# A hybrid decoder block in fp32 on one core: start, eviction, query pass, compressed values, gate terms and residual loads rearranged

## The chip, the core and the metric

The kernel runs on one core of a Trainium2 chip. The metric is the device time of one launch in microseconds (us), the median of several runs. The engines are PE (matrix products), DVE (VectorE), ACT (ScalarE), POOL (GpSimd) and SP (SyncE, which here issues most DMA transfers). PEld is PE's loading of stationary operands, which overlaps its products.

## What is computed

One layer, for a sequence of 1024 rows of 1024 values in fp32:

```python
h = rms_norm(x, norm_mix)
q, kv, g_attn, u_pool, g_merge = split(h @ w_in)   # 512, 768, 24, 512, 2048 columns
a = nsa_attention(q, kv, g_attn, ...) @ w_branch_attn
b = pool_mixer(u_pool, pool_w, pool_scale) @ w_branch_pool
ga, gb = split(sigmoid(g_merge))                    # 1024 each
x = x + (ga * a + gb * b) @ w_out
h = rms_norm(x, norm_mlp)
out = x + square(relu(h @ w_ff1)) @ w_ff2
```

The attention has 8 heads of 64 in 2 key groups and three branches, each with a softmax: over 63 compressed blocks of keys and values, over selected blocks, and over a window of 512 positions; the sum is weighted by gates per head. (With 16 of 16 blocks selected, the selected branch covers all earlier positions.) Queries and keys are rotated (rope).

## The kernel before

Every fp32 operand is split into a high part and a low part (`hi`, and `lo` = operand - `hi`, both float32r), and a product is the sum of three: hi by hi, hi by lo, lo by hi (`mm3`, L74 to L79; which line is which depends on the operand that stays). A tile has 128 partitions; `NT` = `NK` = 8 tiles of tokens and of channels. Weights stream through `load` (L164): a raw tile of 128x512 (256 KB; a ring of `RAWS` = 4), its high part on ACT, its low part on DVE or POOL (rings of `HILO` = 3). The order of instructions on each engine comes from a scheduler that works on the program order.

The stages, by the times of the trace: the first projection (0 to 52, L233 to L254) multiplies the normalised input by 512 key and value columns, eight PSUM banks `acc`, one for each token tile. At its end the banks are evicted (L265 to L271): ACT writes 384 columns to `kvA`, DVE reads the other 128 twice to write the high and low part of the values `vst[0]`. Block 2 (280 more columns) and `compress` follow (to 104); block 2's PSUM tiles take the banks of `acc`, so its first product needs banks that are read out. Then the queries (104 to 158): `qblock(0)` and `qblock(1)`, 256 columns each; each tile is evicted by ACT, rotated by POOL (five operations), and stored to DRAM (`qd`). The rotated keys of a tile are transposed by PE in between. From 158 to 339 come the pooling mixer and the gate products `gb` (to DRAM, `gbd`).

The attention (339 to 706, L512 to L742) runs over 32 pairs of (query tile i, head pair hp). For each, `units_a` makes scores and softmax, `units_b` transposes the probabilities (L652), splits them (ACT L655, DVE L656) and multiplies by values into `oacc` (L663); the last block of each unit is that of the compressed values, `vch`, which has 64 partitions. A pair's `units_b` runs one pair behind. Between these steps stand terms of another product: `ga_terms`, 128 terms of three products each (`psG`), whose sixteen results `z` go to DRAM (`tad`); `advance` gives them out in proportion to the work done. Query tiles come back from `qd` through `load_q` and are transposed and split (`split_q`, L549).

The attention-branch projection (706 to 745 for the first half of the sequence) multiplies `oT` by `w_branch_attn`, reads `tad` and `gbd` back and merges. Then `w_out` (first half 745 to 789, second half to 870): for each of 8 output tiles m two weight tiles, 24 products, and the residual sum on DVE (L820) with `x`, which was loaded straight into `acc[:, m, sl]` (named `accx` in the profile, L817). From 870 on the MLP runs. Besides, POOL's DMA queue makes sums of MLP weights in DRAM during the attention (`wsw_ff`, 1 MB each).

## Time and profile before

| | us |
|---|---|
| median of 3 runs | 1493.94 (1491.46 to 1497.39) |
| the profiled execution | 1493.06 |
| its span | 1491.3 |
| PE busy | 1443.1 (97%) |
| DVE busy | 1006.1 (67%) |
| ACT busy | 759.2 (51%) |
| POOL busy | 154.1 (10%) |

The span runs from the first to the last instruction of the profiled execution; 1.8 us of its time lie outside. Busy PE time contains the tails of products, which overlap the next one, so the distance from one product's start to the next, the pitch, tells more than its duration. A row of the timeline gives start, duration, engine, line, operation, output and inputs, and in brackets the idle time before it and what ended it.

### The profile page before, as it was taken

To read this page: it belongs to the slowest core of one execution; us is meant where nothing else is said; L and a number is where in the kernel's file an instruction comes from. 1 tells how busy PE (TensorE), PEld (TensorE's weight loads), DVE (VectorE), ACT (ScalarE), POOL (GpSimd) and SP (SyncE) were. 2 spreads that over 40 slices of the span, in tenths; PEclk is the share of its full clock that TensorE was granted. 3 is DMA by queue.
4 is the path that set the end of the run, shared out by engine and by line. 5 is a ranking of instruction groups with operands and counts; after the bars stand their busy time and mean duration, and the time that the engine had idled before them with its cause. 6 is when DMAs were issued, how large, how long until landed. Compare 5 with 4: busy or idle time off the path is not lost.

```text
span 1491.3 us, 20797 instructions
## 1 busy us (share of the span) xinstructions
PE 1443.1 (97%) x7385; PEld 1193.7 (80%) x7385; DVE 1006.1 (67%) x1950; ACT 759.2 (51%) x1559; POOL 154.1 (10%) x214
## 2 busy tenths in 40 slices
PE   8899999998999999999899999999999999999996
PEld 6788888886778887787688888888888888888885
DVE  5793461115888888787657658667897376669995
ACT  4454231124778877776334454575344454764451
POOL 2006423331111111111000000000000000000000
PEclk9999999999999999999999999999999999999998
DMA  8234217875768678766955332333233233333323
GB/s 309 69 100 149 71 43 189 215 202 132 201 156 212 153 187 196 171 169 150 327 174 162 108 97 91 100 100 99 85 106 97 94 99 93 99 94 97 98 80 113
DMA packets 130233, 204.67 MB, mean 137 GB/s; under 512 B 9936, under 2 KB 62928, under 8 KB 129616
## 3 DMA queue, kind: packets, MB, share of 16 engines
q1 hardware_dynamic: 112064, 136.22, 29.7%
q0 software_dynamic: 17920, 67.11, 19.9%
q8 instruction: 58, 0.95, 0.2%
q14 instruction: 47, 0.39, 0.1%
q10 hardware_dynamic: 144, 0.00, 0.0%
HBM read 186.52 MB, written 83.89 MB: 181 GB/s over the span
## 4 chain that ended last, share of the span: by engine, by line
PE 87%; DVE 5%; DMA 3%; ACT 2%; issue 1%; POOL 0%; SPq 0%; DVEq 0%; ACTq 0%; POOLq 0%
PE psm L79 16%; PE psm L77 16%; PE psm L78 16%; PE oacc L663 6%; PE psF L78 5%; PE psF L79 5%; PE psF L77 5%; PE psT L652 4%; PE psS L557 3%; PE psS L558 2%; PE psG L77 2%; PE psG L78 2%; PE psG L79 2%; DMA gb<-gbd 1%; PE psS L560 1%
## 5 line engine op out<-in xcount | busy, mean ns | idle before, releaser
L77 PE MATMUL psm<-mv,whi 128*128 128x512 f32 x896 | 350.6, 391 | 0.0
L78 PE MATMUL psm<-mv,whi 128*128 128x512 f32 x896 | 350.6, 391 | 0.0
L79 PE MATMUL psm<-mv,wlo 128*128 128x512 f32 x896 | 350.5, 391 | 0.0
L866 ACT CAST whi<-wraw 128x512 fp32r<-128x512 f32 x224 | 138.9, 621 | 257.6 <-PE psm L78 193.0
L82 DVE TENSOR_TENSOR wlo<-wraw,whi 128x512 fp32r<-128x512 f32 x288 | 196.7, 686 | 90.7 <-ACT whi L866 70.0
L78 PEld LDWEIGHTS psm<-mv,whi 128*128 128x128 f32 x896 | 168.3, 188 | 36.8
L77 PEld LDWEIGHTS psm<-mv,whi 128*128 128x128 f32 x896 | 168.3, 188 | 36.7
L79 PEld LDWEIGHTS psm<-mv,wlo 128*128 128x128 f32 x896 | 168.3, 188 | 36.7
L179 ACT CAST whi<-wraw 128x512 fp32r<-128x512 f32 x112 | 69.7, 622 | 122.2 <-PE psF L78 57.9
L656 DVE TENSOR_TENSOR pl<-psT,ph 128x512 fp32r<-128x512 f32 (+1 forms) x160 | 101.9, 646 | 30.3 <-ACT ph L655 29.0
L655 ACT CAST ph<-psT 128x512 fp32r<-128x512 f32 (+1 forms) x160 | 87.7, 556 | 49.4 <-PE psT L652 47.6
L567 DVE TENSOR_REDUCE nm<-psS 128x1 f32<-128x64 f32 (+8 forms) x192 | 99.8, 539 | 17.4 <-PE psS L560 10.2
L82 POOL TENSOR_TENSOR wlo<-wraw,whi 128x512 fp32r<-128x512 f32 x48 | 65.5, 1367 | 120.3 <-ACT whi L179 100.0
L77 PE MATMUL psF<-xh,whi 128*128 128x512 f32 x192 | 74.7, 389 | 0.0
L78 PE MATMUL psF<-xl,whi 128*128 128x512 f32 x192 | 74.7, 389 | 0.0
L79 PE MATMUL psF<-xh,wlo 128*128 128x512 f32 x192 | 74.7, 389 | 0.0
L568 ACT ACTIVATE pS<-psS,nm 128x64 f32<-128x64 f32 (+8 forms) x128 | 67.9, 532 | 8.8 <-DVE nm L567 8.3
L846 ACT CAST mv<-mt 128x512 fp32r<-128x512 f32 x96 | 59.1, 617 | 15.9 <-DVE mt L844 11.4
L82 DVE TENSOR_TENSOR mv<-mt,mv 128x512 fp32r<-128x512 f32 x96 | 65.0, 684 | 1.1 <-ACT mv L846 0.6
L663 PE MATMUL oacc<-ph,vst 128*128 128x256 f32 x264 | 64.0, 317 | 1.2 <-ACT ph L655 0.9
L652 PE MATMUL psT<-cf,pS 128*128 128x128 f32 x352 | 60.5, 276 | 2.7 <-DVE pS L624 2.6
L77 PE MATMUL psF<-bhi,xh 128*128 128x256 f32 (+1 forms) x192 | 55.6, 293 | 5.7 <-DVE vst L270 4.4
(248 smaller groups left out, 2970.0 us busy)
## 6 DMA issues: line engine op xcount, KB each, us to landing
wraw<-wsw_ff SPq DMA_DIRECT2D x128, 256.0 KB
wraw<-in_w_ff SPq DMA_DIRECT2D x96, 256.0 KB
wsw_ff<-in_w_ff POOLq DMA_DIRECT2D x16, 1024.0 KB, 9.1
wsw_ff<-wsw_ff POOLq DMA_DIRECT2D x16, 1024.0 KB, 9.5
wraw<-in_w_in SPq DMA_DIRECT2D x40, 256.0 KB
wraw<-in_w_out SPq DMA_DIRECT2D x32, 256.0 KB
xt<-in_x SPq DMA_DIRECT2D x8, 512.0 KB
qd<-q SPq DMA_DIRECT2D x16, 256.0 KB
```

Of the source, the lines that this page charges most:

```text
L77: nc.tensor.matmul(ps, lhsT=sh, rhs=mh, start=first and i == 0, stop=False, skip_group_check=more)
L78: nc.tensor.matmul(ps, lhsT=sh, rhs=ml, start=False, stop=False, skip_group_check=more)
L79: nc.tensor.matmul(ps, lhsT=sl, rhs=mh, start=False, stop=last and i == n - 1, skip_group_check=more)
L82: eng.tensor_tensor(lo, src, f(hi), op=SUB)
L179: nc.scalar.copy(h, v)
L567: nc.vector.tensor_reduce(nm, v, axis=AX.X if flat else AX.XY, op=MAX, negate=True)
L568: nc.scalar.activation(p if flat else p.rearrange("p (a n) -> p a n", a=2), v, AF.Exp, bias=nm, accum_out=sm)
L652: nc.tensor.transpose(ps[:, j, e], src[e][:, c0:c0 + P], ident)
L655: nc.scalar.copy(ph[:, :n], ps[:, :n])
L656: nc.vector.tensor_tensor(pl[:, :n], ps[:, :n], f(ph[:, :n]), op=SUB)
L663: nc.tensor.matmul(o, lhsT=v, rhs=part[:rows, j], start=gi == 0 and j == 0 and part is ph, stop=2 * gi + j == nb - 1 and part is pl)
L866: nc.scalar.copy(hi, raw)
```

## The change

- **Start.** Nine products of a constant tile with itself are put at PE's head (L235, into the last bank, which is overwritten later). The weight load of the first channel tile goes out on ACT's DMA queue, so that SP's begins with the input. The low part `wl` is subtracted by DVE, not by POOL.
- **Eviction.** ACT evicts all 512 columns of a bank to `kvA`; DVE makes the values' two parts from `kvA`.
- **Queries.** One `qblock` of 512 columns; seven of its weight tiles in a pool of their own (`qb`), one in the stream's ring. The space is that of `compress`'s tiles, now in a pool `xp` that is closed before. The keys of tile t are rotated and transposed after query tile t. POOL's ropes get buffers of their own.
- **Compressed values.** `vch` has 128 partitions, the upper half zero, so all value products read 128 rows.
- **Attention's start and end.** The first two query tiles are loaded during the pooling stage, into a pool outside (`qp`). `advance` gives 20 terms ahead at once (`FIRST`) and holds 16 back (`LAST`), of which 0.4 x 16 fall to each of the last two pairs.
- **Residual.** `x` is loaded to a tile of the ring `wraw`, which the residual sum reads.

```diff
...
 
-    def rope(eng, v, nh, cos, sin, wk):
+    def rope(eng, v, nh, cos, sin, wk, tag=""):
         cb = cos[:, None, None, :].to_broadcast([P, nh, 2, 8])
         sb = sin[:, None, :].to_broadcast([P, nh, 8])
-        A = wk.tile([P, 8, 2, 8], F32, name="ropeA", bufs=2)[:, :nh]
-        B = wk.tile([P, 8, 2, 8], F32, name="ropeB", bufs=2)[:, :nh]
+        A = wk.tile([P, 8, 2, 8], F32, name="ropeA" + tag, bufs=2)[:, :nh]
+        B = wk.tile([P, 8, 2, 8], F32, name="ropeB" + tag, bufs=2)[:, :nh]
         x = v[:, :, 0:16].rearrange("p h (b e) -> p h b e", b=2)
...
             else:
-                hi = blk.tile([P, 280], F32R, tag="bhi", name="bhi", bufs=10)
-                lo = blk.tile([P, 280], F32R, tag="blo", name="blo", bufs=10)
+                hi = blk.tile([P, n], F32R, tag="bhi", name="bhi", bufs=8 if n < HALF else 7)
+                lo = blk.tile([P, n], F32R, tag="blo", name="blo", bufs=8 if n < HALF else 7)
             v, h, l = raw[:, :w], hi[:, :w], lo[:, :w]
...
     vst = [vk.tile([P, NT, NG, P], F32R, name=f"vst{b}") for b in range(2)]
-    vch = vk.tile([DH, NG, P], F32R, name="vch")
+    vch = vk.tile([P, NG, P], F32R, name="vch")
+    nc.gpsimd.memset(f(vch[DH:P]), 0.0)
     kds = vk.tile([P, NG, NCB + S], F32R, name="kds")
...
         acc = [ps0.tile([P, HALF], F32, name="acc0") for _ in range(NT)]
+        for _ in range(9):
+            nc.tensor.matmul(acc[NT - 1][:, 0:P], lhsT=ones, rhs=ones, start=True, stop=True)
         for k in range(NK):
...
             wl = pa.tile([P, HALF], F32R, name="wl", bufs=3)
-            nc.sync.dma_start(wr, a["w_in"][k * P:(k + 1) * P, C_KC:C_KC + HALF])
+            (nc.scalar if k == 0 else nc.sync).dma_start(wr, a["w_in"][k * P:(k + 1) * P, C_KC:C_KC + HALF])
             if k == 0:
...
             nc.scalar.copy(wh, wr)
-            sub(nc.gpsimd, wl, wr, wh)
             for h in range(2):
...
                                                op0=MUL, op1=SUB)
+                if h == 0:
+                    sub(nc.vector, wl, wr, wh)
             for t in range(NT):
...
             rc = rcol[:, t:t + 1]
-            nc.scalar.activation(kvA[:, t, 0:384], acc[t][:, 0:384], AF.Copy, scale=rc)
-            vv = acc[t][:, 384:512].rearrange("p (g d) -> p g d", g=NG)
-            nc.vector.tensor_scalar(vst[0][:, t, :, 0:DH], vv, rc, None, op0=MUL)
-            nc.vector.scalar_tensor_tensor(vst[0][:, t, :, DH:P], vv, rc, f(vst[0][:, t, :, 0:DH]),
-                                           op0=MUL, op1=SUB)
+            nc.scalar.activation(kvA[:, t], acc[t], AF.Copy, scale=rc)
+            vv = kvA[:, t, 384:512].rearrange("p (g d) -> p g d", g=NG)
+            nc.vector.tensor_copy(vst[0][:, t, :, 0:DH], vv)
+            sub(nc.vector, vst[0][:, t, :, DH:P], vv, vst[0][:, t, :, 0:DH])
 
...
         wkA = pool(st, "wkA", side="right")
+        xctx = ExitStack()
+        xp = pool(xctx, "xp", side="right")
 
         def compress(kv):
-            X = wkA.tile([P, 16, NG, NCB], F32, name="X")
-            Xh = wkA.tile([P, 16, NG, NCB], F32R, name="Xh")
-            Xl = wkA.tile([P, 16, NG, NCB], F32R, name="Xl")
+            X = xp.tile([P, 16, NG, NCB], F32, name="X")
+            Xh = xp.tile([P, 16, NG, NCB], F32R, name="Xh")
+            Xl = xp.tile([P, 16, NG, NCB], F32R, name="Xl")
             nc.gpsimd.memset(X[DH:P, :, :, NCB - 1:NCB], 0.0)
...
                 for g in range(NG):
-                    nc.vector.tensor_copy(vch[:, g], f(vh[g * DH:(g + 1) * DH]))
+                    nc.vector.tensor_copy(vch[0:DH, g], f(vh[g * DH:(g + 1) * DH]))
 
...
 
-        def qblock(b):
-            w = block_w(b * 256, 256)
+        def qblock():
+            w7 = load(cols(a["w_in"], C_Q, HALF, 0, 7), nc.vector, qb)
+            w1 = load(cols(a["w_in"], C_Q, HALF, 7, 1), nc.vector)
+            w = [Parts(w7[e].tiles + w1[e].tiles) for e in range(2)]
             for t in range(NT):
...
                 ps = psF.tile([P, HALF], F32, name="psF")
-                mm3(ps[:, :256], [(XH[k][:, sl], XL[k][:, sl], w[0][:, k], w[1][:, k])
-                                  for k in range(NK)])
-                q = wkA.tile([P, 4, 2, DH], F32, name="q", bufs=2)
-                nc.scalar.activation(q, dup(ps[:, :256].rearrange("p (h d) -> p h d", d=DH)), AF.Copy,
-                                     scale=req[:, t:t + 1])
-                rope(nc.gpsimd, q.rearrange("p h e d -> p (h e) d"), 8, cosT[:, t], sinT[:, t], wkA)
-                nc.sync.dma_start(qd[t][:, b * 512:(b + 1) * 512], q.rearrange("p h e d -> p (h e d)"))
-                if b == 0:
-                    keys(t, 0, kds[:, :, NCB + t * P:NCB + (t + 1) * P])
-                elif t in (2, 5):
+                mm3(ps, [(XH[k][:, sl], XL[k][:, sl], w[0][:, k], w[1][:, k]) for k in range(NK)])
+                for b in range(2):
+                    q = wkA.tile([P, 4, 2, DH], F32, name="q", bufs=2)
+                    nc.scalar.activation(q, dup(ps[:, b * 256:(b + 1) * 256].rearrange("p (h d) -> p h d", d=DH)),
+                                         AF.Copy, scale=req[:, t:t + 1])
+                    rope(nc.gpsimd, q.rearrange("p h e d -> p (h e) d"), 8, cosT[:, t], sinT[:, t], wkA, "q")
+                    nc.sync.dma_start(qd[t][:, b * 512:(b + 1) * 512], q.rearrange("p h e d -> p (h e d)"))
+                keys(t, 0, kds[:, :, NCB + t * P:NCB + (t + 1) * P])
+                if t in (2, 5):
                     hf = t // 3
...
         nc.vector.tensor_scalar(sg, sg, 0.5, 0.5, op0=MUL, op1=ADD)
-        qblock(0)
-        qblock(1)
+        xctx.close()
+        qb = pool(st, "qb", side="right")
+        qblock()
         dump("kds", f(kds))
...
 
+    qctx = ExitStack()
+    qp = pool(qctx, "qp")
+
+    def load_q(i, g):
+        qi = qp.tile([P, HALF], F32, name="qi", bufs=2)
+        nc.sync.dma_start(qi, qd[i][:, g * HALF:(g + 1) * HALF])
+        return qi
+
 
...
                 prev = cur
+            qi = [load_q(0, 0), load_q(0, 1)]
             for m in range(NK):
...
 
-        def load_q(i, g):
-            qi = wk.tile([P, HALF], F32, name="qi", bufs=2)
-            nc.sync.dma_start(qi, qd[i][:, g * HALF:(g + 1) * HALF])
-            return qi
-
         def split_q(qi):
...
             i, hp, g, nw, w0 = (u[n] for n in ("i", "hp", "g", "nw", "w0"))
-            blocks = [(u["pS"], NCB + b * P, vst[0][:, b, g], P) for b in range(i + 1)]
-            blocks += [(u["pW"], b * P, vst[1][:, w0 + b, g], P) for b in range(nw // P)]
-            blocks.append((u["pS"], 0, vch[:, g], NCB))
+            blocks = [(u["pS"], NCB + b * P, vst[0][:, b, g]) for b in range(i + 1)]
+            blocks += [(u["pW"], b * P, vst[1][:, w0 + b, g]) for b in range(nw // P)]
+            blocks.append((u["pS"], 0, vch[:, g]))
             o = oacc[:, hp % 2]
...
                 ps = psT.tile([P, HALF], F32, name="psT").rearrange("p (b e n) -> p b e n", b=2, e=2)
-                for j, (src, c0, _, _) in enumerate(bl):
+                for j, (src, c0, _) in enumerate(bl):
                     for e in range(2):
...
                 for part in (ph, pl):
-                    for j, (_, _, v, rows) in enumerate(groups[gi]):
-                        nc.tensor.matmul(o, lhsT=v, rhs=part[:rows, j], start=gi == 0 and j == 0 and part is ph,
+                    for j, (_, _, v) in enumerate(groups[gi]):
+                        nc.tensor.matmul(o, lhsT=v, rhs=part[:, j], start=gi == 0 and j == 0 and part is ph,
                                          stop=2 * gi + j == nb - 1 and part is pl)
...
 
-        LAG = 1
+        LAG, FIRST, LAST = 1, 20, 16
         fill = ga_terms()
...
         total, nterm = sum(weight), 2 * NK * NK
-        done, given, summed = 0.0, 0, 0
+        done, given, summed, ending = 0.0, 0, 0, 0.0
 
         def advance(w):
-            nonlocal done, given
+            nonlocal done, given, ending
             done += w
-            while given < nterm and given < nterm * done / total:
+            if len(bseq) and n >= len(pairs) - 1:
+                ending += 0.4 * LAST / nslot
+            while given < nterm and given < FIRST + (nterm - FIRST - LAST) * done / total + ending:
                 next(fill, None)
...
 
-        qi = load_q(0, 0)
-        q = split_q(qi)
-        qnext = load_q(0, 1)
+        q = split_q(qi[0])
+        qnext = qi[1]
         bseq, bw = [], 0
...
     psTctx.close()
+    qctx.close()
     attn.close()
...
                 wh, wl = load(cols(a["w_out"], m * P, P), nc.vector)
-                nc.sync.dma_start(acc[:, m, sl], a["xT"][m * P:(m + 1) * P, sl])
+                xt = strm.tile([P, HALF], F32, tag="wraw", name="wraw", bufs=RAWS)
+                nc.sync.dma_start(xt, a["xT"][m * P:(m + 1) * P, sl])
                 ps = bank()
                 mm3(ps, [(wh[:, k], wl[:, k], mg[k][0], mg[k][1]) for k in range(NK)])
-                nc.vector.scalar_tensor_tensor(acc[:, m, sl], ps, 0.5, acc[:, m, sl], op0=MUL, op1=ADD)
+                nc.vector.scalar_tensor_tensor(acc[:, m, sl], ps, 0.5, xt, op0=MUL, op1=ADD)
                 square_into(sqs, acc[:, m, sl], m == NK - 1, sqa)
```

On ACT at the end of the first projection, where the scheduler places the casts of `load` (L179; `bhi` for block 2, `whi` for compress) around the evictions. Before:

```order
L123 ACTIVATE rs_sq<-rs_ms 128x8
L245 CAST wh<-wr 128x512
L179 CAST bhi<-wraw 128x280 x8
L179 CAST whi<-wraw 128x512 x3
L267 ACTIVATE kvA<-acc_155,rcol 128x384
```

Now:

```order
L248 CAST wh<-wr 128x512
L179 CAST bhi<-wraw 128x280 x8
L179 CAST whi<-wraw 128x512 x2
L271 ACTIVATE kvA<-acc_156,rcol 128x512
L179 CAST whi<-wraw 128x512
L271 ACTIVATE kvA<-acc_157,rcol 128x512
```

The third compress weight's cast moved from ahead of the first eviction to behind it; 384 columns became 512. The other banks' evictions follow in a row in both.

On PE at the attention's start (`psF` is the last product of the pooling stage, `psG` a gate term, `psS` scores, `psT` transposes; `cf` holds the identity, `cb` the mask). Before:

```order
L77 MATMUL psG<-xh_67,whi 128x512
L78 MATMUL psG<-xl_75,whi 128x512
L549 MATMUL psT<-cf,qi 128x128 x4
L79 MATMUL psG<-xh_67,wlo 128x512
L77 MATMUL psG<-xh_68,whi 128x512
L78 MATMUL psG<-xl_76,whi 128x512
L79 MATMUL psG<-xh_68,wlo 128x512
L557 MATMUL psS<-kds,qh 128x192
L557 MATMUL psS<-kdw,qh 128x128
L558 MATMUL psS<-kds,ql 128x192
```

Now, first:

```order
L79 MATMUL psF<-mxh,wlo 128x512
L77 MATMUL psG<-xh_65,whi 128x512
L568 MATMUL psS<-kds,qh 128x192
L568 MATMUL psS<-kdw,qh 128x128
L568 MATMUL psS<-kds,qh 128x192
L569 MATMUL psS<-kds,ql 128x192
L571 LDWEIGHTS cb
L571 MATMUL psS<-cb 128x64
```

and, 34 rows on, behind 22 more gate products:

```order
L77 MATMUL psG<-xh_72,whi 128x512
L78 MATMUL psG<-xl_80,whi 128x512
L79 MATMUL psG<-xh_72,wlo 128x512
L663 MATMUL psT<-cf,pS 128x128 x2
L663 MATMUL psT<-cf,pW 128x128 x2
L568 MATMUL psS<-kds,qh 128x192
L569 MATMUL psS<-kds,ql 128x192
L77 MATMUL psG<-xh_65,whi 128x512
L78 MATMUL psG<-xl_73,whi 128x512
```

The first query transposes (L549, now L560) are gone from here, to a place just behind the query stage. The scores stand ahead of the gate terms, and the transposes of the first probabilities behind eight of them; 21 terms stand ahead of the first value product, where there were five and a part.

On SP in the output products' first half (`accx` and the `wraw` from `in_xT` are the residual; `ta`, `gb` are merge operands). Before:

```order
L178 DMA wraw<-in_w_out 128x4x128
L804 DMA gb<-gbd_1_111 128x512
L178 DMA wraw<-in_w_out 128x4x128
L803 DMA ta<-tad_1_129 128x512
L804 DMA gb<-gbd_1_113 128x512
L803 DMA ta<-tad_1_131 128x512
L178 DMA wraw<-in_w_out 128x4x128
L817 DMA accx<-in_xT 128x512 x2
L178 DMA wraw<-in_w_out 128x4x128
L817 DMA accx<-in_xT 128x512 x2
```

Now:

```order
L831 DMA wraw<-in_xT 128x512
L816 DMA ta<-tad_1_130 128x512
L178 DMA wraw<-in_w_out 128x4x128
L817 DMA gb<-gbd_1_114 128x512
L816 DMA ta<-tad_1_132 128x512
L178 DMA wraw<-in_w_out 128x4x128
L831 DMA wraw<-in_xT 128x512
L178 DMA wraw<-in_w_out 128x4x128 x2
L831 DMA wraw<-in_xT 128x512
L178 DMA wraw<-in_w_out 128x4x128 x2
L831 DMA wraw<-in_xT 128x512
L178 DMA wraw<-in_w_out 128x4x128 x2
```

Eight residual loads stood ahead of the first row shown, now one; the others went out in pairs behind one weight tile, now one behind each two.

## Rows read from the trace of the kernel before

**Rows 1.** Four stages: length, busy PE, PEld, DVE, ACT, POOL (instructions), clock, DMA, GB/s:
```profile
104.16:158.35 54.19, 50.54 (x413) 48.78 (x411) 21.17 (x93) 23.12 (x55) 28.41 (x78) 1.00 0.43 132
...
339.26:360.00 20.74, 14.86 (x75) 11.88 (x73) 8.20 (x33) 8.64 (x34) 1.28 (x1) 0.84 0.49 126
...
400.00:706.00 306.00, 301.83 (x1977) 246.49 (x1975) 247.63 (x534) 230.37 (x542) 48.00 (x54) 1.00 0.75 176
706.00:745.20 39.20, 31.57 (x118) 24.15 (x118) 24.73 (x42) 14.84 (x27) 1.53 (x2) 0.91 1.07 319
```

**Rows 2.** Timeline of the hand-off: start, duration, engine, line, operation, [idle before <-releaser]:
```profile
51.16 3.87 ACT L267 ACTIVATE kvA<-acc,rcol 128x384 f32<-128x384 f32 x8
...
56.58 0.38 PE L77 MATMUL psF<-bhi,xh 128*128 128x280 f32 x1 [4.35 <-DVE vst L270]
```

**Rows 3.** Timeline of the start:
```profile
4.32 1.25 POOL L82 TENSOR_TENSOR wl<-wr,wh 128x512 fp32r<-128x512 f32 x1 [3.38 <-ACT wh L245]
4.36 1.50 DVE L249 TENSOR_SCALAR xh<-xr,gmix 128x512 fp32r<-128x512 f32 x1 [4.36 <-DMA xr<-in_xT]
...
6.01 3.23 PE L77 MATMUL acc<-wh,xh 128*128 128x512 f32 x7 [6.01 <-DVE xh L249]
...
6.56 0.48 DVE L249 TENSOR_SCALAR xh<-xr,gmix 128x512 fp32r<-128x512 f32 x1
```

**Rows 4.** Timeline of PE at the attention's start:
```profile
339.04 0.39 PE L78 MATMUL psF<-mxl,whi 128*128 128x512 f32 x1
339.26 0.39 PE L79 MATMUL psF<-mxh,wlo 128*128 128x512 f32 x1
340.49 0.50 PE L77 MATMUL psG<-xh,whi 128*128 128x512 f32 x1 [0.84 <-DVE gb L503]
...
346.65 0.90 PE L549 MATMUL psT<-cf,qi 128*128 128x128 f32 x4 [4.02 <-DMA qi<-qd]
...
347.77 0.63 PE L77 MATMUL psG<-xh,whi 128*128 128x512 f32 x1
348.19 0.63 PE L78 MATMUL psG<-xl,whi 128*128 128x512 f32 x1
```

**Rows 5.** Timeline of DVE, a residual sum in the output products:
```profile
751.49 0.69 DVE L820 SCALAR_TENSOR_TENSOR accx<-psm,accx 128x512 f32<-128x512 f32 x1 [1.58 <-PE psm L79]
```

**Rows 6.** Three loads in the chain of waits: start, duration, what:
```profile
47.01 3.61 DMA wraw<-in_cmp_k_w
...
339.68 6.92 DMA qi<-qd
...
730.80 5.05 DMA wraw<-in_w_out
```

**Rows 7.** Timeline of PE in the query stage:
```profile
119.30 0.28 PE L77 MATMUL psF<-bhi,xh 128*128 128x256 f32 x1
119.42 0.28 PE L78 MATMUL psF<-blo,xh 128*128 128x256 f32 x1
...
135.73 0.39 PE L77 MATMUL psF<-bhi,xh 128*128 128x256 f32 x1 [1.37 <-ACT bhi L179]
```

**Rows 8.** Timeline of PE around the compressed values of one unit:
```profile
462.09 0.40 PE L663 MATMUL oacc<-pl,vst 128*128 128x256 f32 x2
462.42 0.38 PE L663 MATMUL oacc<-ph,vch 64*128 64x256 f32 x1
462.65 0.27 PE L663 MATMUL oacc<-pl,vch 64*128 64x256 f32 x1
462.85 0.50 PE L77 MATMUL psG<-xh,whi 128*128 128x512 f32 x1
463.18 0.40 PE L78 MATMUL psG<-xl,whi 128*128 128x512 f32 x1
```

**Rows 9.** Timeline of PE in the attention-branch projection:
```profile
735.69 0.51 PE L79 MATMUL psm<-oh,wlo 128*128 128x512 f32 x1 [3.38 <-DVE wlo L82]
```

**Rows 10.** Transfers issued from 690 to 760: count, KB each:
```profile
accx<-in_xT SPq DMA_DIRECT2D x16, 256.0 KB
```

## The prediction

> **What bounds the kernel now.** I read the busy table by stage first. The matmul engine (PE) is busy for nearly all of the span, so a change saves time only where it removes an idle stretch of PE, runs PE faster, or takes work from it. The idle stretches lie in few places: the attention's first 20.74 us hold 14.86 us of PE work, the attention-branch projection's 39.20 us hold 31.57, the query stage's 54.19 hold 50.54 [rows 1]. Before the queries stands one more hole, between the first projection's last matmul and the next at 56.58, which waited 4.35 us [rows 2]. The attention's body (400 to 706) is PE work at 301.83 of 306.00, but VectorE (DVE) is busy there for 247.63, so an engine in second place is not far behind [rows 1]. Then I read, for each of these places, the timeline for the wait that ends last and the pace of the matmuls around it. The MLP behind 870 isn't touched; I cost it at nothing.
>
> **First projection and its eviction.** The first matmul starts at 6.01, behind an xh product of 1.50 us on DVE; the same product alone takes 0.48. In that stretch GpSimd (POOL) ran a low part for 1.25 us. The first seven matmuls take 3.23 us, 0.46 each, twice the later pace [rows 3, 4]. After the change the low part is a DVE subtraction (0.69 us, by the residual's pass over a tile of the same size [rows 5]), the x halves are at the head of SP's queue, and nine constant products run while loads land. I expect real matmuls from about 4.7 instead of 6.01, at the faster pace; 0.3 to 1.7 us. For each k step DVE now carries 2 xh, 2 xl and one low part, about 3 us, against 24 matmuls of 0.23, 5.5 us, so PE stays the bound.
>
> At the hand-off the first matmul of block 2 waited for DVE to read PSUM a second time for token tile 6; eight ScalarE (ACT) evictions of 384 columns took 3.87 us in the meantime [rows 2]. Now ACT evicts 512 columns, about 0.6 each instead of 0.48, and a bank is free when ACT is done; block 2's first bank is the one of tile 5. One cast of a compress weight still stands between the first two evictions, and its load landed only after 3.61 us at 50.62 in the trace [rows 6]. So: 51.3 + 5 x 0.6 = 54.3 instead of 56.58. The start and this share one limit (that load), so I take them together at **-2.5 us** (0 to -4; the far end if the shorter pause also leaves the matmuls behind it at full pace).
>
> **Queries in one pass.** 384 matmuls of 256 columns at 0.12 become 192 of 512 at 0.225 [rows 4, 7]: 45.5 - 43.5 = 2 us. Of the 3.65 us idle [rows 1], the largest is a wait for a weight cast, 1.37 [rows 7], and others are for rotated keys: the ropes now have 5.5 us per tile instead of 2.8, and the casts are eight, not sixteen. Against it: the eight low parts now cost DVE 0.69 each instead of about 0.42 in a stretch in which it is busy with ropes, 2.2 us more before the first query matmul can end. **-4 us** (-1 to -5.5).
>
> **Attention's start.** PE waited 0.84 us for the last gate, then 4.02 us for the query tile, whose load was issued only when the stage began and took 6.92 us; behind it the products run at 0.43 [rows 4, 6]. Now both loads and the first split stand far ahead, the scores come first, and 20 gate terms (60 matmuls, 13.8 us) stand before the first softmax results are needed. The 0.84 stays. Of the 5.88 us idle and some 2.5 us lost to pace in these 20.74 us [rows 1], I take **-6 us** (-3 to -8).
>
> **Compressed values at 128 rows.** The product with vch uses 64 rows of the array. In a unit, two pl products of 256 columns are followed after 0.33 us instead of 0.24, the two vch products after 0.23 and 0.20 instead of 0.12, and the next gate product takes 0.33 instead of 0.23 [rows 7, 8]. That is 0.09 + 0.11 + 0.08 + 0.10 = 0.38 us per unit, x 32 units = 12.2 us. Padded, all products have one shape. Bounds: 0 if the change of operand and not of row count costs the time, 12.2 if it all goes and PE sets the pace everywhere. In the first 8 units DVE and ACT set it, so 24 units: **-9 us**.
> By the Trainium skill ("TensorE: Matmul & The Clock Gate", Part 3, "The mechanism") a weight load overlaps a running matmul only when the two differ in the row groups that they use. By that, 64-row and 128-row neighbours would be no worse off than two of 128 rows, and this term would be 0. The rows don't bear it out: neighbours of equal rows follow each other at 0.12, those of unlike rows at 0.2 and more.
>
> **Fewer gate terms in the body.** 20 of 128 terms go to the start and some 16 to the end, so 36 x 0.69 = 25 us of cover leave the body. With vch its PE work falls from about 302 to 275 us (400 to 706, by share), while DVE's 247.63 stays but for a few low parts [rows 1]: 90% instead of 81%, and in a pipeline of dependent steps some waits must come. **+5 us** (0 to +14).
>
> **Attention's end and branch projection.** PE waited first for the casts of the attention's result, and 3.38 us at 735.69 for a weight's low part [rows 9], whose load took 5.05 us [rows 6]. All 16 residual loads of 256 KB were in the queue between 690 and 760 [rows 10]; 8 of them were issued before the first output product at 745. Now the last 16 gate terms cover the first casts, and residual tiles wait in the ring of weight tiles, so only two or three are loaded by then: some 1.4 MB less of what moves at about 320 GB/s [rows 1], 4.4 us, of a stage with 7.63 us idle and about 3 at the slower pace. **-6 us** (-2 to -10).
>
> **Output products.** Each m now takes three of four ring tiles (two weights, one residual), so weight a of block m waits for the residual sum of block m-2. That sum ends 0.9 us after its block, a block lasts 24 x 0.2275 = 5.46 us, the cast takes 0.62: a load has about 3.8 us. In the trace a lone load took about 3.6, one under contention 5.05 [rows 6]. **+1.5 us** (0 to +14).
>
> **Sum** -2.5 - 4 - 6 - 9 + 5 - 6 + 1.5 = -21 us against the profiled execution's 1493.06 (span 1491.3 and 1.8 around it): 1472. The median of the runs shown, 1493.94, lies 0.9 above it: **1473 us**.
>
> **Rivals.**
> 1. Compressed values gain nothing (the page's rule, or the change of operand costs the time): -12 instead of -21, 1482. For: 0.10 of the 0.38 lies on a gate product that doesn't read vch. Against: the pitch inside the vch pair itself, 0.23, where nothing but the row count is unlike the queries' 0.12 [rows 7, 8].
> 2. DVE becomes the bound of the body. Then the gain of vch there and of the 25 us moved is partly given back, +14 instead of +5: 1482. For: DVE at 81% now. Against: PE idles for 4.17 of the 306.00 us now, with the same chains behind it [rows 1].
> 3. The ring stalls the output products. It decides from a load time of 3.8 us on; if each load took what the query tile took, 6.92 [rows 6], 14 blocks would lose 3.1 us each, 43 us: 1473 - 1.5 + 43 = 1515, slower than before. For: a load of 5.05 in the neighbouring stage. Against: that stage moves 319 GB/s, the output stage 146 [rows 1], and the bigger traffic (gate loads) has gone by then.
> 4. The change doesn't do what it says: with the scheduler moving gate terms elsewhere, start and end gain little, -21 + 8 = -13, 1481.
>
> **How the numbers follow.** Forecast 0.6 (1464 to 1480); rival 1 0.13, rival 2 0.12, rival 4 0.07, rival 3 0.08 (0.04 of it past 1501, the rest between). A measurement of this kernel tells about 0.5%, 7.5 us, from no change: faster below 1486.5. The cases below that hold 0.88 less some overlap of rivals 1, 2 and 4 that would land at 1487 to 1495: faster 0.86, same 0.10, slower 0.04. Range 1460 to 1487: down to where vch gives 12 and the ends their bounds, up to two rivals together.
>
> **What the profile after would show.** First real matmul before 5.5; block 2's first matmul waiting for ACT's kvA, under 3 us; the query stage near 50 us; no wait for qi, and psG matmuls at 0.23 from the stage's first; vch products pitched at 0.12; DVE near 90% in the body with PE waits on DVE; the branch stage near 33 us; output blocks 5.5 us apart. It is wrong if vch products keep 0.2 or more, if output blocks are over 6 us apart with waits on a weight cast, or if the body's PE idle exceeds 14 us.

## The result

The changed kernel takes 1477.89 us (median of 4 runs, 1475.16 to 1480.62) against 1493.16 for the kernel before (4 runs, 1491.46 to 1497.39); the ratio is 0.9894, 95% interval 0.9864 to 0.9923. The forecast was 1473 with a range of 1460 to 1487. The profiled execution's span went from 1491.3 to 1478.2, 13.1 us, where the sum of the terms was 21. So the direction holds and the time lies in the range, but two terms, the attention and its end, were far off.

Stages, by the start of the first product of each (us). "Attention" runs from the first gate term to the last value product, "branch" from there to the first output product, "rest" to the end of the span:

| | to block 2 | block 2, compress | queries | pooling | attention | branch | rest |
|---|---|---|---|---|---|---|---|
| before | 56.58 | 47.58 | 54.19 | 182.14 | 365.09 | 34.09 | 751.63 |
| changed | 54.33 | 48.65 | 49.50 | 182.49 | 360.33 | 31.95 | 750.95 |
| difference | -2.25 | +1.07 | -4.69 | +0.35 | -4.76 | -2.14 | -0.68 |

The stages of the changed kernel, in the columns of [rows 1]:

```profile
102.98:152.48 49.50, 49.27 (x225) 38.31 (x223) 21.04 (x85) 19.24 (x44) 25.30 (x72) 1.00 0.44 139
152.48:332.00 179.52, 178.66 (x787) 146.97 (x786) 58.52 (x75) 41.28 (x65) 59.34 (x61) 1.00 0.58 148
332.00:695.50 363.50, 349.47 (x2294) 287.01 (x2292) 291.07 (x679) 271.65 (x688) 55.65 (x63) 0.99 0.74 176
695.50:727.25 31.75, 26.06 (x97) 20.65 (x97) 19.43 (x33) 10.02 (x18) 1.53 (x2) 0.85 0.93 264
```

The query stage has no idle time left (49.27 busy of 49.50; it was 50.54 of 54.19). The branch stage still holds 26.06 us of work in 31.75, and the attention has 14 us without work. (The branch row of [rows 1] runs to 745.20, one block into the output products, whose first product stood at 739.67; by the bounds of the table the branch stage before was 34.09, not 39.20.)

At the start and at the hand-off (PE's pause between the first projection and block 2) the timeline of PE now reads:

```profile
6.20 1.20 PE L77 MATMUL acc<-wh,xh 128*128 128x512 f32 x4 [1.32 <-ACT wh L248]
...
54.33 0.60 PE L77 MATMUL psF<-bhi,xh 128*128 128x280 f32 x1 [4.14 <-ACT kvA L271]
```

Real products begin no earlier than before (6.20 against 6.01 in [rows 3]), but at four in 1.08 us (the next starts at 7.28) instead of seven recorded ones in 3.07 (the next started at 9.08). The reason for their start changed: xh was done early, and the weight, now on ACT's queue, landed last. The hand-off waits on ACT's eviction, as the forecast said, and still lasts 4.14 us, where it named under 3. The chain of waits leads to the load of the third compress weight and the five evictions behind its cast:

```profile
46.60 4.14 DMA wraw<-in_cmp_k_w
...
51.38 2.91 ACT kvA L271 x5
```

Behind this pause block 2 runs at the lower of the clock's two levels, 1.2 GHz. The stretch at its start, first of the changed kernel, then of e4_accx (below), whose hand-off took 0.96 us (the clock is the third number from the end, 1.00 for 2.4 GHz):

```profile
54.33:58.00 3.67, 3.67 (x16) 3.67 (x16) 2.06 (x10) 1.41 (x3) 0.46 (x1) 0.50 0.11 30
```

```profile
52.80:56.00 3.20, 3.20 (x25) 3.20 (x26) 2.04 (x10) 1.39 (x3) 0.45 (x1) 1.00 0.12 34
```

Of all thirteen profiles, seven show the lower clock there, with hand-offs of 1.8 to 4.4 us, and block 2 with compress takes 47.6 to 48.7; six stay at 1.00, with hand-offs of 0.9 to 2.0 us, and take 46.0 to 46.6.

In the attention the first value products and the compressed ones:

```profile
353.66 0.48 PE L674 MATMUL oacc<-ph,vst 128*128 128x256 f32 x2
...
354.56 0.37 PE L674 MATMUL oacc<-ph,vch 128*128 128x256 f32 x1
354.77 0.28 PE L674 MATMUL oacc<-pl,vch 128*128 128x256 f32 x1
354.88 0.39 PE L77 MATMUL psG<-xh,whi 128*128 128x512 f32 x1
355.11 0.39 PE L78 MATMUL psG<-xl,whi 128*128 128x512 f32 x1
```

From the second vch product to the gate term 0.11, from that to the next 0.23: the edge of [rows 8] (0.20 and 0.33) is gone. (The 0.21 behind the first vch product follows on a transpose.)

The end of the attention is where the changed kernel loses. PE's timeline, and the stage row of the last two units, first of the changed kernel, then of the kernel before:

```profile
665.73 0.40 PE L79 MATMUL psG<-xh,wlo 128*128 128x512 f32 x1
667.88 0.41 PE L568 MATMUL psS<-kdw,qh 128*128 128x320 f32 x1 [1.75 <-ACT pS L579]
...
683.89 2.28 PE L663 MATMUL psT<-cf,pS 128*128 128x128 f32 x8 [0.89 <-DVE pS L635]
```

```profile
665.20:695.40 30.20, 25.05 (x140) 20.52 (x139) 20.57 (x41) 17.74 (x36) 3.08 (x4) 0.83 0.68 157
```

```profile
677.40:705.60 28.20, 27.89 (x178) 23.21 (x177) 20.99 (x42) 18.38 (x39) 3.07 (x4) 1.00 0.61 143
```

The last gate term stands at 665.73, 30 us ahead of the last value product: the 16 terms held back in the program were not issued last. The last two units (a unit is one of the 32 pairs of query tile and head pair) had one term instead of 12, and still took 30.2 us instead of 28.2: PE waits, and the granted clock falls from 1.00 to a mean of 0.83.

The branch stage's longest wait, and the two longest loads in its chain of waits:

```profile
722.82 0.79 PE L79 MATMUL psm<-oh,wlo 128*128 128x512 f32 x1 [4.59 <-DVE wlo L82]
```

```profile
703.71 5.58 DMA gb<-gbd
...
711.88 9.10 DMA ta<-tad
```

The wait of [rows 9], 3.38 us, has become 4.59, with gate loads of 5.6 to 9.1 us ahead of it. The output products' residual sums, on DVE, follow each other every 5.49 us:

```profile
749.80 0.69 DVE L834 SCALAR_TENSOR_TENSOR accx<-psm,wraw 128x512 f32<-128x512 f32 x1 [1.63 <-PE psm L79]
...
755.29 0.69 DVE L834 SCALAR_TENSOR_TENSOR accx<-psm,wraw 128x512 f32<-128x512 f32 x1 [1.63 <-PE psm L79]
```

So the ring of four tiles with three users per block costs nothing in sum. (In the second half one block comes after 6.32 us and the next after 4.17, where the kernel before has 5.42 and 5.34.)

### The profile page after: what moved, and what is told of

Same layout as the page of the kernel before. It is cut to its first block, busy times and chain, and to the rows that moved or that the text cites. A ratio compares the mean times of both kernels' runs of the same rounds, so it can differ in the third digit from the quotient of the medians.

```text
span 1478.2 us, 20415 instructions
## 1 busy us (share of the span) xinstructions
PE 1436.6 (97%) x7211; PEld 1184.2 (80%) x7211; DVE 1007.9 (68%) x1950; ACT 758.3 (51%) x1551; POOL 143.8 (10%) x207
## 4 chain that ended last, share of the span: by engine, by line
PE 81%; DVE 6%; DMA 5%; ACT 3%; POOL 2%; issue 2%; SPq 0%; DVEq 0%; ACTq 0%; POOLq 0%
PE psm L79 16%; PE psm L77 16%; PE psm L78 16%; PE oacc L674 5%; PE psT L663 4%; PE psF L78 4%; PE psF L77 4%; PE psF L79 4%; PE psS L568 3%; PE psS L569 2%; PE psG L77 2%; PE psG L78 2%; PE psG L79 2%; DMA xt<-in_x 1%; DMA ta<-tad 1%
## 5 line engine op out<-in xcount | busy, mean ns | idle before, releaser
L179 ACT CAST whi<-wraw 128x512 fp32r<-128x512 f32 x113 | 70.2, 622 | 124.8 <-PE psF L78 59.0
L663 PE MATMUL psT<-cf,pS 128*128 128x128 f32 x352 | 63.6, 287 | 5.8 <-DVE pS L635 5.6
L674 PE MATMUL oacc<-pl,vst 128*128 128x256 f32 x264 | 58.2, 300 | 2.6 <-DVE pl L667 2.3
```

The costliest lines, as they stand in the source:

```text
L179: nc.scalar.copy(h, v)
L663: nc.tensor.transpose(ps[:, j, e], src[e][:, c0:c0 + P], ident)
L674: nc.tensor.matmul(o, lhsT=v, rhs=part[:, j], start=gi == 0 and j == 0 and part is ph, stop=2 * gi + j == nb - 1 and part is pl)
```

## The experiments

Each is the changed kernel with one edit, unless said otherwise. Medians of four to ten runs beside runs of the kernel before, whose own median was 1494.08 beside e1 to e4, 1495.37 beside e5 to e8 and 1496.70 beside e9 to e11; across these groups the ratio is the fairer measure. Stages are read from one profile each, as in the table above.

| | median us | ratio to before (95%) | to block 2 | queries from | attention | branch |
|---|---|---|---|---|---|---|
| changed | 1477.89 | 0.9894 (0.9864 to 0.9923) | 54.33 | 102.98 | 360.33 | 31.95 |
| e1_vch64 | 1486.14 | 0.9946 (0.9927 to 0.9966) | 51.82 | 98.28 | 369.43 | 31.43 |
| e2_hold_all | 1496.63 | 1.0009 (0.9996 to 1.0023) | 52.42 | 98.59 | 376.11 | 34.80 |
| e3_ga_even | 1472.94 | 0.9848 (0.9825 to 0.9871) | 52.89 | 100.80 | 352.73 | 32.30 |
| e4_accx | 1477.34 | 0.9889 (0.9859 to 0.9918) | 52.79 | 99.09 | 359.51 | 30.14 |
| e5_before_qi | 1493.68 | 0.9988 (0.9976 to 1.0000) | 56.60 | 105.26 | 363.13 | 33.15 |
| e6_start_old | 1478.83 | 0.9898 (0.9876 to 0.9920) | 54.13 | 100.12 | 360.50 | 32.96 |
| e7_evict_old | 1479.05 | 0.9901 (0.9874 to 0.9928) | 53.45 | 100.06 | 359.08 | 31.28 |
| e8_even_poollo | 1474.95 | 0.9865 (0.9842 to 0.9889) | 53.82 | 101.63 | 352.58 | 32.00 |
| e9_first0 | 1472.25 | 0.9831 (0.9796 to 0.9867) | 52.62 | 100.32 | 351.60 | 33.86 |
| e10_even_sums | 1467.63 | 0.9807 (0.9772 to 0.9842) | 53.43 | 99.96 | 354.09 | 26.06 |
| e11_best | 1468.45 | 0.9811 (0.9782 to 0.9840) | 53.93 | 102.51 | 355.63 | 26.07 |

**Compressed values back on 64 rows.**

```diff
-    vch = vk.tile([P, NG, P], F32R, name="vch")
-    nc.gpsimd.memset(f(vch[DH:P]), 0.0)
+    vch = vk.tile([DH, NG, P], F32R, name="vch")
...
-                        nc.tensor.matmul(o, lhsT=v, rhs=part[:, j], ...
+                        nc.tensor.matmul(o, lhsT=v, rhs=part[:rows, j], ...
```

> The changed kernel with the compressed values back on 64 rows. Theory (an edge between 64-row and 128-row products costs PE 0.38 us per unit): the attention, 360.4 us in the changed kernel from the first gate term to the last value product, gets 6 to 12 us longer, the vch pair is pitched at 0.23 and 0.20 again, the whole 1484 to 1490. Rival (the row count costs nothing where PE isn't the bound): within 2 us of the changed kernel's 1478.

The attention is 9.10 us longer, the whole 8.2. PE's timeline shows the edges again, at the same place in the program as the rows of the changed kernel above:

```profile
350.22 0.38 PE L673 MATMUL oacc<-ph,vch 64*128 64x256 f32 x1
350.44 0.28 PE L673 MATMUL oacc<-pl,vch 64*128 64x256 f32 x1
350.65 0.50 PE L77 MATMUL psG<-xh,whi 128*128 128x512 f32 x1
350.99 0.40 PE L78 MATMUL psG<-xl,whi 128*128 128x512 f32 x1
```

0.21 and 0.34 where the padded form has 0.11 and 0.23. The theory holds, rival 1 of the prediction falls. Of the 9.10 us, 1.3 lie in the first eight units and 7.8 in the other 24, 0.32 each.

**Gate terms tied to their place, and gate terms even.** The first ties every term behind the last value product ahead of it in the program (`last[0]` below is the value product traced last); the second gives the terms out as before the change and is called the even kernel below.

```diff
-                next(fill, None)
+                if last[0] is not None:
+                    with tc.issue_after(getattr(last[0], "ins", last[0])):
+                        next(fill, None)
+                else:
+                    next(fill, None)
...
```

```diff
-        LAG, FIRST, LAST = 1, 20, 16
+        LAG, FIRST, LAST = 1, 0, 0
```

> The changed kernel with every gate term tied, in PE's order, behind the last value product that stands ahead of it in the program, so that the terms can't be drawn ahead of their place. Theory (in the changed kernel the terms meant for the end were drawn forward, so that the last two units had one term between them, PE idled and its clock fell): the last 28 us get 20 terms and lose their waits, attention 360 becomes 350 to 355, the whole 1468 to 1473. Rival (DVE bounds the body; where terms stand makes no difference): attention 358 to 362, the whole 1476 to 1480; if the terms drawn forward had filled waits of the body, longer than the changed kernel.

> The changed kernel with FIRST = 0 and LAST = 0: gate terms given out evenly as before, all else as changed. Theory (20 terms at the start save 8 us there, and their lack at the end costs about as much): within 3 us of the changed kernel, attention 357 to 363, with six terms in each of the last two units and no fall of the clock there, and the waits of the start back. Rival (the early block is worth its 8 us in net): 1484 to 1488.

The two kernels differ from the changed one in where the 128 terms stand (e1_vch64, above, does not). How far the attention is when so many units are done (us behind its first gate term; in brackets the terms issued by then):

| units done | 4 | 8 | 28 | 30 | 32 |
|---|---|---|---|---|---|
| before | 34.5 (11.3) | 64.4 (24) | 304.9 (104) | 336.9 (116) | 365.1 (128) |
| changed | 36.2 (26.3) | 65.7 (39.7) | 299.7 (116) | 330.2 (127) | 360.3 (128) |
| e1_vch64 | 37.1 (26.3) | 67.0 (39.7) | 307.0 (116) | 338.6 (127) | 369.4 (128) |
| e2_hold_all | 36.4 (24) | 67.7 (30) | 308.8 (95) | 341.8 (104) | 376.1 (125) |
| e3_ga_even | 24.0 (8) | 52.8 (17.7) | 294.2 (104) | 325.4 (116) | 352.7 (128) |
| e9_first0 | 23.8 (8) | 53.1 (17.7) | 285.3 (91.3) | 317.1 (102) | 351.6 (125) |

A term is three products at 0.23, 0.69 us. Up to unit 4 the changed kernel takes 36.2 - 26.3 x 0.69 = 18.1 us without its terms, the even one 24.0 - 5.5 = 18.5, the kernel before 26.7. So the block of 20 terms covers nothing that isn't covered without it. In the last two units the changed kernel takes 30.1 us with one term, the even one 27.3 with 12, which alone are 8.3 us: 10.4 us lost there against 2.8 gained up to unit 30 (242.6 without terms, against 245.4). The stage row of the even kernel's last two units, to be held against 665.20 of the changed one:

```profile
658.20:685.60 27.40, 26.98 (x179) 22.69 (x177) 20.60 (x42) 18.70 (x39) 3.07 (x4) 1.00 0.73 173
```

So the theory on the lack at the end holds, and its balance was misjudged: 7.6 us of the attention and 5 of the whole, not an even trade. (Four profiles with even terms have an attention of 352.6 to 355.6 us, four with the changed kernel's terms and padded products 359.1 to 360.5.)

Tying the terms was expected to give an attention of 350 to 355 us and gave 376.1. Its waits of PE over the attention, and those of the changed kernel (total, times, longest):

```profile
PE psT L663 <- DVE pS L635: 9.6, 14, 1.7
PE oacc L674 <- DVE pl L667: 4.7, 15, 0.6
PE oacc L674 <- ACT ph L666: 3.3, 10, 0.4
```

```profile
PE psT L663 <- DVE pS L635: 5.6, 8, 1.1
PE oacc L674 <- DVE pl L667: 2.3, 8, 0.4
...
PE oacc L674 <- ACT ph L666: 0.8, 2, 0.5
```

The starved end is mended (two units with 21 terms in 34.3 us), but the terms, free to be drawn forward, had filled waits for the softmax and the probabilities all along. The sum of these waits grew by 9 us; the rest of the 15.8 us isn't accounted for by them. About 7 us of the loss lie in units 5 to 8, which had 6 terms instead of 13.4 and ran at a granted clock of 0.84 (1.00 in the changed kernel):

```profile
366.97:398.30 31.33, 27.75 (x162) 22.64 (x163) 24.08 (x76) 23.26 (x79) 4.38 (x5) 0.84 0.67 158
```

**Nothing at the start, 16 held back.** The counter-test to the tie: terms free, but the supply of each place given by the program.

```diff
-        LAG, FIRST, LAST = 1, 20, 16
+        LAG, FIRST, LAST = 1, 0, 16
```

> The changed kernel with FIRST = 0 and LAST = 16: no block of terms at the start, 16 held back for the end, so the units in between get fewer than in the even kernel (91 instead of 104 ahead of unit 28). Theory (the body's units take the same time with fewer terms, since DVE and ACT set their pace once PE has too little to do): no more than 2 us gained up to unit 28 against the 294 us of the even kernel, the last four units longer by what the 10 more terms take, 7 us; attention 356 to 361. Rival (the terms cost PE time wherever they are): attention 352 to 354, as the even kernel.

The row of the table is clear: 12.7 terms fewer up to unit 28 save 8.9 us against the even kernel, 0.70 each; 9.7 more in the last four units cost 7.8, and the last three terms fall behind the last value product, into the branch stage (33.86). The rival holds: in the body a term costs PE's time; DVE, busy for about 83% there, isn't the bound with 91 terms by unit 28. Held-back terms alone do no harm: the whole is that of the even kernel within the noise. What starves the end is the block at the start, behind which the scheduler ran through the supply: by unit 28 the program has given out 95 terms in the changed kernel (where the tied kernel stands) and 91 in this one; PE had issued 116 there and 91.3 here. Why the scheduler draws the terms so far forward only with the block isn't shown.

**The early query tile alone.** The kernel before with this one edit, which loads the tile in the pooling stage:

```diff
...
+            qi = [load_q(0, 0), load_q(0, 1)]
             for m in range(NK):
...
-        qi = load_q(0, 0)
-        q = split_q(qi)
-        qnext = load_q(0, 1)
+        q = split_q(qi[0])
+        qnext = qi[1]
```

> The kernel before with one part of the change alone: the first two query tiles loaded in the pooling stage, into a pool outside, gate terms given out as before. Theory (the gain at the attention's start is the early query tile's, and the block of 20 terms added nothing to it): the first value product comes 6 to 8 us after the first gate term instead of 16.5, the attention gets 6 to 9 us shorter than 365.1, the whole 1485 to 1488. Rival (the tile is early, but without a block of terms PE waits for the softmax instead): 1490 to 1494.

The first value product comes 6.72 us behind the first gate term, where it came 16.54 behind:

```profile
341.30 0.50 PE L77 MATMUL psG<-xh,whi 128*128 128x512 f32 x1 [0.84 <-DVE gb L512]
...
348.02 0.45 PE L666 MATMUL oacc<-ph,vst 128*128 128x256 f32 x2
```

Up to unit 4 it needs 24.6 - 5.5 = 19.1 us without terms, 7.6 less than before. But over the attention only 2.0 us of that are left, and over the whole 1.7: at unit 12 4.7 us of it are there, at unit 24 none. The theory on the mechanism holds and its price falls: the time was given back in units 12 to 24, which took 115.9 us without terms, against 111.2 before and 110.5 in the even kernel, whose value products are padded. Why is open; another profile with even terms and padded products (e11_best) has 113.7 in these units, so some of it can be chance. The rival's time came, but not its wait: PE's longest wait for the softmax in the first four units is 1.0 us.

**Start and eviction as before.** Two kernels:

```diff
-        for _ in range(9):
-            nc.tensor.matmul(acc[NT - 1][:, 0:P], lhsT=ones, rhs=ones, start=True, stop=True)
...
-            (nc.scalar if k == 0 else nc.sync).dma_start(wr, ...
+            nc.sync.dma_start(wr, ...
             nc.scalar.copy(wh, wr)
+            sub(nc.gpsimd, wl, wr, wh)
...
-                if h == 0:
-                    sub(nc.vector, wl, wr, wh)
```

```diff
-            nc.scalar.activation(kvA[:, t], acc[t], AF.Copy, scale=rc)
-            vv = kvA[:, t, 384:512].rearrange("p (g d) -> p g d", g=NG)
+            nc.scalar.activation(kvA[:, t, 0:384], acc[t][:, 0:384], AF.Copy, scale=rc)
+            vv = acc[t][:, 384:512].rearrange("p (g d) -> p g d", g=NG)
...
```

> The changed kernel with the start as before: no constant products, all first loads on SP with the weight ahead, the low part wl on POOL. Theory (the start is worth 2 us at the end of the first projection, of which the hand-off, bound by a compress weight's load, gives part back): last product of the projection near 51.5 instead of 49.4 to 49.8, the whole 0 to 3 us above 1478. Rival (the pace of the first products counts in full): 2 to 4 us above.

> The changed kernel with the eviction as before (ACT 384 columns, DVE two passes over PSUM). Theory (the load of the third compress weight sets the hand-off in both): hand-off 4 to 5.5 us long, block 2's first product waiting on DVE's second pass, the whole 0 to 2 us above 1478. Rival (DVE's passes over PSUM set it): the hand-off 2 us longer than in runs of the changed eviction, the whole 2 to 4 above.

Each alone is within 1.2 us of the changed kernel, which the measurement can't tell from nothing. With the old start the projection's last product came at 52.30 (49.4 to 51.7 in the profiles with the new one), and the hand-off was 1.4 us (0.9 to 4.1): what the start gains, the hand-off can take. With the old eviction the hand-off was 1.4 us too, not the expected 4 to 5.5. In both, as in the changed kernel, the chain of waits leads to the load of a compress weight, first with the old start, then with the old eviction:

```profile
45.42 3.96 DMA wraw<-in_cmp_k_w
```

```profile
44.53 4.30 DMA wraw<-in_cmp_k_w
```

The nine profiles with both parts new have the first query product between 98.28 and 102.98, median 100.3; the two with both old have it at 104.16 and 105.26. So the two may together be worth about 4 us, but that isn't shown: the two kernels with both old also lack the change's other parts, and no run undoes both alone. The profile of the changed kernel shown above was the latest of the nine at this point.

**Residual loaded straight into accx.**

```diff
-                xt = strm.tile([P, HALF], F32, tag="wraw", name="wraw", bufs=RAWS)
-                nc.sync.dma_start(xt, a["xT"][m * P:(m + 1) * P, sl])
+                nc.sync.dma_start(acc[:, m, sl], a["xT"][m * P:(m + 1) * P, sl])
```

> The changed kernel with the residual loaded straight into accx again. Theory (the residual loads took transfer time from the branch projection): the branch stage, 31.8 us in the changed kernel, gets 2 to 5 us longer with more loads of xT ahead of the output products; the whole 1480 to 1483. Rival (the stage is bound by gate, weight and sum transfers alone, the residual's fill gaps): within 1 us of 1478.

The branch got 1.8 us shorter, not longer, with six residual loads in it instead of two. The theory falls: these loads took nothing that the stage lacked. The whole is the same.

**What bounds the branch.** Gate terms even in both; in the first the low parts of the branch weights on POOL, in the second the sums of MLP weights made earlier.

```diff
-                wh, wl = load(cols(a["w_branch_attn"], m * P, P, 0, 4), nc.vector)
+                wh, wl = load(cols(a["w_branch_attn"], m * P, P, 0, 4))
```

```diff
-            if n >= 2 and summed < 25 * done / total:
+            if n >= 2 and summed < 32 * done / total:
```

> Gate terms given out evenly (FIRST = LAST = 0), and the low parts of the branch projection's weights on POOL, which computes nothing there. Theory (in the changed kernel a weight's low part stood in DVE's queue behind a merge that waited 4.82 us for a gate load): no PE wait over 1 us in the branch stage, the stage 30.4 us becomes 25 to 28, the whole 1467 to 1470. Rival (the gate loads bound the stage, whatever PE waits for): the stage with the first output products lasts as long, 1472 to 1474.

> Gate terms evenly (FIRST = LAST = 0), and the sums of MLP weights made earlier in the attention (32 instead of 25 over its course), so that none moves during the branch projection. Theory (each sum moves 1 MB twice there, and the gate loads of 256 KB take 7 to 11 us beside it): the branch stage 30.4 becomes 24 to 27, no wait of PE over 2 us in it, the whole 1467 to 1470. Rival (the in-order queue of loads and few merge buffers bound it): 29 to 31.

With POOL the stage took 32.00 us, where 25 to 28 were expected and the even kernel has 32.30. The wait only moved (PE's waits in the branch stage; the longest of the even kernel is 3.0, on DVE):

```profile
PE psm L79 <- POOL wlo L82: 4.2, 1, 4.2
```

Behind it POOL waited for the high part on ACT, and ACT for a merge that waited for gate loads. The sums did it. The stage rows of the even kernel with the sums late and with the sums early, what moved in it when they were late, and a gate load in its chain of waits then:

```profile
687.46:717.86 30.40, 26.74 (x97) 20.50 (x98) 18.15 (x29) 8.68 (x16) 1.53 (x2) 0.85 1.02 290
```

```profile
688.02:712.19 24.17, 23.95 (x96) 19.29 (x97) 19.33 (x31) 9.88 (x17) 0.00 (x0) 0.93 0.81 259
```

```profile
ta<-tad SPq DMA_DIRECT2D x8, 256.0 KB
gb<-gbd SPq DMA_DIRECT2D x8, 256.0 KB
wraw<-in_w_out SPq DMA_DIRECT2D x4, 256.0 KB
wsw_ff<-wsw_ff POOLq DMA_DIRECT2D x1, 1024.0 KB, 11.9
...
wsw_ff<-in_w_ff POOLq DMA_DIRECT2D x1, 7.1
```

```profile
703.50 8.48 DMA gb<-gbd
```

6.2 us less in the stage, 5.3 in the whole, and PE is busy for 23.95 of 24.17. The last sum moves 1 MB twice, a copy within DRAM in 7.1 us and an addition in 11.9, and the addition of the sum before it, issued at 683.72, still ran at the stage's start. Beside them the gate loads were slow, and behind these stood the merges, the casts and the weights in the queues. Which of the transfers slowed them most isn't separated.

**Both.** The same with the residual straight into accx:

> The same with the residual loaded straight into accx again. Theory (the ring made SP's queue wait; the residual's transfers weren't what the stage lacked): the branch stage another 1 to 2 us shorter, the whole 1465 to 1469. Rival (the residual's transfers take the room that the sums left): longer than with the ring by 1 to 3 us.

1468.45 against 1467.63 with the ring, branch 26.07 against 26.06: no difference, so neither the theory nor the rival holds. The even terms with early sums, 1467.63 (0.9807, 0.9772 to 0.9842), are, with this kernel, the fastest of all that were run: 10 us below the changed kernel, 0.9 points by the ratio.

## Why the prediction was right, and where it was not

- **Start and hand-off, -2.5 (0 to -4): right in size.** Block 2 came 2.25 us earlier. The step to "real products from about 4.7" failed: real products begin at 6.20, since the weight, sent on another queue, landed after the input and became the last wait (1.32 us on wh). What was won is the pace of the first products (the 0.46 of the prediction counts the last one's tail; from start to start they were 0.44 apart). The sum for the hand-off, 54.3, is met by this profile to 0.03 us, but by luck: in the nine profiles with both parts new block 2 starts between 51.82 and 54.33. The shared limit, the load of a compress weight, stands in the chain of waits of the changed kernel and of both kernels with one part undone, and undoing one costs nothing clear of noise. The forecast's far end, full pace behind a shorter pause, didn't come in this profile: block 2 ran at half the clock, and block 2 with compress took 1.07 us longer, a stretch for which the forecast had no term.
- **Queries, -4 (-1 to -5.5): right**, -4.69, and 49.5 in every run of the changed form (no run undoes this part alone). The split was not: PE's work fell by 1.3 us and its idle time by 3.4. (By the paces that the prediction gives, 384 x 0.12 and 192 x 0.225 make 46.1 - 43.2 = 2.9, not 2.) The extra DVE time for wider low parts left one wait of 0.2 us on `blo`.
- **Compressed values, -9 (0 to -12.2): right.** Undone, the attention took 9.10 us more. Reading the pitch at the edges gave the mechanism; paying 0.38 for 24 of 32 units gave the price only in sum: those 24 units gave 0.32 each, and the first eight, counted at nothing, 1.3.
- **Attention's start, -6 (-3 to -8): the mechanism right, the price half right, and the block of terms misjudged.** The early tile takes 7.6 us from the first four units; alone, in the kernel before, 2.0 are left at the end. The 20 terms, which I counted as the cover for the softmax, cover nothing.
- **Body, +5 (0 to +14): the size near by luck, the mechanism wrong.** I expected waits on DVE in a body with fewer terms. The body had no fewer: the scheduler drew them forward, 116 by unit 28 instead of the 104 of the kernel before and the 95 of the program. The cost came in the last two units, 10.4 us, 7.6 net of the 2.8 gained ahead of them. The step that failed is "some 16 to the end": I took the places of the terms from the program's text, where in PE's order 134 products stand between the last gate term and the last value product. That order was there to be read to its end ahead of the forecast. Rival 2 (DVE bounds the body) falls with the kernel that holds 16 back: a term removed from the body saves its full 0.70 us. Rival 4, the scheduler moving terms elsewhere, is what happened, at the end alone: 10.4 us there against the 8 that it was given.
- **Attention's end and branch, -6 (-2 to -10): too much.** 2.14 came, by the bounds of the table. The row that I rested on (16 residual loads in the queue) was true and beside the point; the wait was set by gate loads beside a sum of MLP weights. That sum stood in the trace of before, on POOL's queue, and I hadn't costed it.
- **Output products, +1.5 (0 to +14): nothing lost**, 5.49 us a block but for one of 6.32 that the next made up. Rival 3 falls.

Together the attention gave 4.76 instead of 10 and the branch 2.14 instead of 6: 9 us missing of the sum, offset by 2 us at the output products and behind. That the time still lies in the range owes to the range's width and to these small gains, not to the terms of the attention.

## What to carry to other kernels

Where a scheduler places the work, look up in its order where filler stands against the last work that it is to cover; a count in the program says only how much is available, and a generous block early can empty the supply late. Filler that may move has a use in each small wait, so don't nail it down; limit how much is on offer. When a stage waits for small loads, look for large transfers on other queues in the same stretch before the loads that stand in the same queue.

## What the runs showed of the hardware

- A product of 256 columns on 64 rows next to products on 128 rows makes the edges slower: 0.20 to 0.34 between starts where equal rows have 0.11 to 0.23. Padding with zeros to 128 rows, which doubles the rows of the operand, saved 9.1 us over 64 such products. The rule of the Trainium skill cited in the prediction ("TensorE: Matmul & The Clock Gate", Part 3, "The mechanism"), by which a weight load overlaps a running product only when their row groups differ, would have the padded form no faster; the measurement decides against it for this pattern.
- A sum in DRAM (a copy of 1 MB in 7.1 us, an addition of 1 MB in 11.9, and the end of the addition before) beside loads of 256 KB cost a stage of 24 us another 6.2, though the mean rate was 290 GB/s with it and 259 without.
- With two units short of filler the granted clock fell to a mean of 0.83 over 30 us; those units took longer with one term in them (30.1 us) than with 12 (27.3).
- Profiles of the same code up to there differ by up to 4.7 us at the first query product (98.28 to 102.98): by 2.5 in when block 2 starts, and by 2.5 in block 2 and compress, with the granted clock at 0.50 for the first of its products or at 1.00 throughout. What is gained ahead of there has to be judged over several profiles.
